# Which chunks of the down projections are done by seven products, and when h is read back

## The chip, the cores and the metric

The kernel runs on one core of a Trainium2 chip. The metric is the device time of one launch in microseconds, the median of several runs. A profile belongs to one execution; its span runs from the first to the last instruction of the core. Engines in the profile are PE (TensorE, matmuls; PEld is its weight load), DVE (VectorE), ACT (ScalarE), POOL (GpSimd) and SP (SyncE, which issues most DMAs).

## The reference

Two layers over x of 256 rows and 1024 columns, all in f32. Each layer is a half-step FFN, a mixer, and a second half-step FFN:

```
def swiglu(h, w_gate, w_up, w_down):
    return (jax.nn.silu(h @ w_gate) * (h @ w_up)) @ w_down

for i in range(DEPTH):                                   # DEPTH = 2, D_MODEL = 1024, D_FF = 2816, SEQ = 256
    h = rmsnorm(x, ffn1_norm[i])
    x = x + 0.5 * swiglu(h, ffn1_w_gate[i], ffn1_w_up[i], ffn1_w_down[i])
    h = rmsnorm(x, mix_norm[i])
    proj = h @ w_in[i]                                   # then self attention (chunked in layer 0,
    ...                                                  # differential in layer 1) and memory attention
    x = x + jnp.concatenate([o_s, o_m], axis=-1) @ w_out[i]
    h = rmsnorm(x, ffn2_norm[i])
    x = x + 0.5 * swiglu(h, ffn2_w_gate[i], ffn2_w_up[i], ffn2_w_down[i])
```

The change is in the FFNs alone. A stage is named (layer, FFN): (0,1), (0,2), (1,1), (1,2).

## The kernel before

**Matmuls in three passes.** Every f32 operand is split into a rounded high part and the rest. `dense` (L503) issues for each product hi·xh (L511), lo·xh (L514, the low part of the weights) and hi·xl (L517), each of 128x512. So each piece of a weight needs a cast on ACT (`hi`, L338, `split_hi`) and a subtraction on VectorE (`lo`, L356, `split_lo`) before TensorE can use it.

**Weights.** `loader` issues the weight DMAs on SP (L294), in the order of use, into three raw buffers. A raw buffer is free again when `split_lo` has read its last piece. The split pieces go to four hi/lo slots, which are free when the last product on them is issued. Items are numbered: in stage (0,2), before and after alike, `lo79` to `lo89` are the eleven chunks 0 to 10 of the down weights, and `lo90` begins the next stage. raw and hi/lo numbers of one chunk differ (raw82 feeds chunk 9, `lo88`).

**The FFN.** Eleven blocks of 256 hidden columns are made first (gate and up, tiles `gu`). `evac` turns each into h: silu on ACT (L633), the product on VectorE (L636), a transpose (L644) into `hb`; then h is written to DRAM (L650, `hd`) and read back in another layout (L656, `hr`), both on SP. A plain chunk splits `hr` into `ht` by a cast (L665) and a subtraction (L667).

**The down stage** has NG = 11 chunks of 256 rows of w_down. Chunks 0 to 7 are taken one by one into four accumulators (`acc00` to `acc11`: two row blocks by two column halves). Chunks 8, 9 and 10 are then taken quarter by quarter: all of acc00 first, so that `finish` (L606) can add it to x while the next quarter runs. In a quarter, TensorE takes two pieces of each chunk, for the first quarter the first and the third.

**Seven products.** A plain chunk is 8 products, 24 matmuls. A chunk listed in `SEVEN` for its stage (L377) is done by a Strassen-like scheme of seven products, 21 matmuls. That needs
- on the weights (`seven_item`, L389): four differences `wsum` on VectorE (L350), seven hi casts and seven lo subtractions in place of four of each. The first seven chunk of a stage uses two hi/lo slots. The later ones are "guests", which put three of their pieces into `gxh`/`gxl`, tiles that belong to the activations elsewhere; one guest at a time;
- on h (`seven_forms`, L672): four small sums `sf` (L681), three casts (L690) and three subtractions (L694). From the third seven of a stage on, they wait in the plan until TensorE has come to the second one;
- after the last seven chunk (`seven_sums`, L710): four of the products have gone into PSUM banks `m1`, `m5`, `m6`, `m7` over all seven chunks of the stage. One copy on ACT (L725, `msum<-m1`), then four additions to x (L714) and four sums (L719) on VectorE bring them into x.

**Who sets the order.** A planner (class Flow) runs when the kernel is built. Threads (`evac`, `split_hi`, `split_lo`, `seven_sums`, ...) yield planned times or conditions, and the instruction that comes due first by its costs is written next. The schedule is manual: each engine runs its instructions in just this order, and waits only for what they need. So a change of the table reorders every engine's queue after it.

Of the kernel before, what the change touches and what calls it, by code (L numbers as in the profile page):

```python
# [26 lines left out]
NG = FF // 256  # L27
# [115 lines left out]
def kernel(  # L143
# [13 lines left out]
    flow = Flow()  # L157
# [125 lines left out]
    def add_chunk(parts, uses=8, w=1):  # L283
        return Item([add_raw(parts)], uses, w)
# [89 lines left out]
    def rows2(w, r):  # L374
        return [(lambda raw: k2(raw), w[r * 256:(r + 1) * 256, :].rearrange("(k p) n -> p k n", p=P))]

    SEVEN = {(0, 1): (), (0, 2): (1, 4, 7), (1, 1): (1, 4, 7), (1, 2): (1, 4, 7)}  # L377
    PAIR = {(0, 1): 4, (0, 2): 3, (1, 1): 3, (1, 2): 3}

    def turned2(w, r):  # L380
        src = w[r * 256:(r + 1) * 256, :].rearrange("(k b i) n -> b i k n", k=2, b=4)
        return [((lambda raw, b=b: k2(raw)[b::4]), src[b]) for b in range(4)]
# [6 lines left out]
    def seven_item(it, guest):  # L389

        r = [it.own(q) for q in range(4)]
        t = lambda j: lambda: it.t[j]
        it.n, it.uses, it.takes, it.gives, it.guest = 1 if guest else 2, 7, 4, 4, guest
        it.sums = [(r[1], r[0]), (r[3], t(0)), (r[3], r[1]), (r[2], t(1))]
        it.units = [(r[0], 0, 1, None), (r[2], 1, 1, None), (r[3], 2, 1, None)] + [(t(j), 3 + j, 1, j) for j in range(4)]
# [46 lines left out]
    def plan_ffn(l, nm, wg, wu, wd):  # L442
# [34 lines left out]
        for c in range(NG):  # L477
            dn.append(add_chunk(turned2(wd[l], c)))
            if c in SEVEN[l, nm]:
                seven_item(dn[-1], c != SEVEN[l, nm][0])  # L480
            elif c >= NG - 3:
# [136 lines left out]
    def ffn(l, nm, xt, gc_next):  # L618
        hts = [None] * NG
        htt = [None] * NG  # L620
        sv = SEVEN[l, nm]
        prog = [-1]

        def evac(g, ps, end, gives=None):


            hb = None
            for tb in range(2):
                yield lambda: end[tb] is not None and xt.rt[tb] is not None
                yield end[tb]  # L630
                yield g2.has(3)
                sil = g2.take([P, 256], F32, "sil")
                nc.scalar.activation(sil, ps[tb][:, 0:256], AF.Silu, scale=xt.r[tb])  # L633
                yield flow.act(256)
                h = g2.take([P, 256], F32, "h")
                nc.vector.scalar_tensor_tensor(out=h, in0=ps[tb][:, 256:512], scalar=xt.r[tb], in1=sil,  # L636
                                               op0=ALU.mult, op1=ALU.mult)
                t = flow.dve(256, 0.06)
                g2.give()
                (gives or (banks, banks))[tb].give()  # L640
                if hb is None:
                    hb = g2.take([P, 4, 2, 2, 32], F32, "hb")
                yield t
                nc.vector.transpose(out=hb[:, :, tb].rearrange("p b f j -> p f b j"),  # L644
                                    in_=h.rearrange("p (f b i) -> p f b i", f=2, b=4))
                t = flow.dve(256, 0.05)
                g2.give()
            yield t
            hd = dram.tile([4, 32, 4, P], F32, tag="hd", name="hd")
            nc.sync.dma_start(out=hd.rearrange("a i b x -> (a i) (b x)"), in_=hb.rearrange("p b t f j -> p (b t f j)"))  # L650
            yield flow.now + 3.0
            g2.give()
            yield flow.now + 2.0
            yield g2.has()
            hr = g2.take([P, 4, P], F32, "hr")
            nc.sync.dma_start(out=hr, in_=hd.rearrange("a i b x -> (i b) a x"))  # L656
            yield flow.now + 6.5
            src = hr.rearrange("p a (c j) -> p c a j", c=4)
            if g in sv:
                yield from seven_forms(g, src)  # L660
                return
            yield g4.has()
            ht = g4.take([P, 2, 4, P], F32R, "ht")
            hi, lo = (ht[:, i].rearrange("p c (a j) -> p c a j", a=4) for i in range(2))
            nc.scalar.copy(out=hi, in_=src)  # L665
            yield flow.act(512)
            nc.vector.tensor_sub(lo, src, hi.bitcast(F32))  # L667
            t = flow.dve(512)
            g2.give()
            hts[g], htt[g] = ht, t  # L670

        def seven_forms(g, src):  # L672


            yield lambda: g4.left >= 2 and g2.left >= 4 and (sv.index(g) < 2 or prog[0] >= sv[1])
            ht = [g4.take([P, 8, P], F32R, "h7") for _ in range(2)]
            sf = g2.take([P, 4, P], F32, "sf")
            s1, s2, s3, s4 = (sf[:, j].rearrange("p (a j) -> p a j", a=4) for j in range(4))
            for op, o, x, y in ((nc.vector.tensor_add, s1, src[:, 2], src[:, 3]), (nc.vector.tensor_sub, s2, s1, src[:, 0]),
                                (nc.vector.tensor_sub, s3, src[:, 0], src[:, 2]), (nc.vector.tensor_sub, s4, src[:, 1], s2)):  # L680
                op(o, x, y)  # L681
                t = flow.dve(P, 0.06)
            yield t
            view = lambda x: x.rearrange("p c (a j) -> p c a j", a=4)
            parts = ((slice(0, 2), src[:, 0:2], view(ht[0][:, 0:2]), view(ht[1][:, 0:2])),
                     (slice(2, 3), src[:, 3:4], view(ht[0][:, 2:3]), view(ht[1][:, 2:3])),
                     (slice(3, 7), sf, ht[0][:, 3:7], ht[1][:, 3:7]))
            ts = []
            for js, x, hi, lo in parts:
                nc.scalar.copy(out=hi, in_=x)  # L690
                ts.append(flow.act(P * (js.stop - js.start)))
            for (js, x, hi, lo), t in zip(parts, ts):
                yield t
                nc.vector.tensor_sub(lo, x, hi.bitcast(F32))  # L694
                t = flow.dve(P * (js.stop - js.start))
            g2.give(2)
            hts[g], htt[g] = ht, t
# [52 lines left out]
        def plain_chunk(g, c, tbs, ks=range(4)):  # L750
            if g not in open_:
                flow.until(banks.has(2))
                open_[g] = [bank(f"gu{tb}", (P, 512)) for tb in range(2)], [None, None]
                flow.spawn(evac(g, *open_[g]))
            ps, end = open_[g]
            for tb in tbs:
                for k in ks:
                    kk = 4 * c + k
                    t = dense(ps[tb], xt.h[tb][:, kk, :], xt.l[tb][:, kk, :], lambda: xt.t[tb][kk],
                              plan[l, nm, "gu"][g, c], k, kk == 0, kk == KT - 1)  # L760
                if c == 1 and 3 in ks:
                    end[tb] = t
# [60 lines left out]
        def product(m):  # L823

            name, left = {"m1": ("b11", (0, 0)), "m5": ("t1", 0), "m7": ("t3", 2), "m6": ("t2", 1), "m3": ("b22", 3),
                          "m2": ("b21", (0, 1)), "m4": ("t4", (1, 1))}[m]
            flow.until(banks.has())
            pb[m] = bank("pair_" + m, (P, 512))
            if m == "m1":
                flow.spawn(pair_sums())  # L830
                for e in range(2):
                    flow.spawn(evac(pair + e, pps[e], pend[e], (g2, g2)))
            for k in range(4):
                if isinstance(left, int):
                    flow.until(lambda: xt.ft[left] is not None)
                    f = xt.fm[left]
                    fh, fl, ready = f[:, 0, k, :], f[:, 1, k, :], lambda: xt.ft[left]
                else:
                    tb, kk = left[0], 4 * left[1] + k
                    fh, fl, ready = xt.h[tb][:, kk, :], xt.l[tb][:, kk, :], lambda: xt.t[tb][kk]  # L840
                t = dense(pb[m], fh, fl, ready, pit[name], k, k == 0, k == 3)
            mt[m] = t
            if m == "m3":
                g4.give(4)
# [874 lines left out]
```

## Time and profile before

| | |
|---|---|
| median of 3 runs | 955.35 us (955.19 to 955.69) |
| profiled execution | 955.69 us, of which the span is 953.9 us |
| mean granted TensorE clock | 1.000 |
| down stage (0,2) begins | 432.70 us after the span's start |
| down stage (1,1) begins | 609.4 us |
| down stage (1,2) begins | 892.3 us |
| SP waiting for VectorE to free a raw buffer | 417.5 us, 110 times |

Times inside the span are counted from its first instruction. A row of the timeline has the start in us, the duration of one instruction or of a run of xN alike instructions, the engine, the line, the operation, out<-in by the program's names, and in brackets the idle time before it with what ended it. VectorE and TensorE start an instruction before the one ahead of it has ended, so a rate is read from start to start, not from a duration.

### The profile page before, as it was taken

The numbers are of one execution on the slowest core, as the hardware profiler recorded it, in microseconds if no ns is written. First come the engines' busy times: TensorE is split into PE (matmuls) and PEld (weight loads), VectorE is DVE, ScalarE is ACT, GpSimd is POOL, SyncE is SP. The second block draws the span as 40 slices with busy tenths as digits, with TensorE's granted clock in tenths as the row PEclk, the third lists the DMA queues.
The fourth block names the chain that finished last, engine by engine and source line by source line (L and its number), as shares of the span: only waits on it lengthen the run. The fifth ranks groups of instructions, "written<-read, shape, count | busy, mean of one in ns | idle before, by whom it ended". The sixth has DMA issues, their size and how long they took to land.

```text
span 953.9 us, 13334 instructions
## 1 busy us (share of the span) xinstructions
PE 945.6 (99%) x4475; PEld 774.1 (81%) x4475; DVE 820.0 (86%) x1483; ACT 587.0 (62%) x1121; POOL 109.1 (11%) x160
## 2 busy tenths in 40 slices
PE   9999999999999999999999999999999999999998
PEld 7888888887777888888888888888787778888886
DVE  7898978888777899979889899796999888999884
ACT  6556566677676746647546656564676865665650
POOL 1000057621210100000000000000434200000000
PEclk9999999999999999999999999999999999999999
DMA  8987799486525387887746679775641367588751
GB/s 265 289 263 236 224 354 296 158 276 210 177 90 177 97 266 225 262 287 219 245 146 219 208 226 288 247 253 166 196 158 57 121 214 228 183 275 276 239 197 45
DMA packets 169887, 204.04 MB, mean 214 GB/s; under 512 B 10137, under 2 KB 145114, under 8 KB 169818
## 3 DMA queue, kind: packets, MB, share of 16 engines
q1 hardware_dynamic: 169498, 202.78, 66.0%
q8 instruction: 35, 0.57, 0.3%
q10 hardware_dynamic: 320, 0.40, 0.1%
q14 instruction: 34, 0.28, 0.1%
HBM read 188.99 MB, written 14.16 MB: 213 GB/s over the span
## 4 chain that ended last, share of the span: by engine, by line
PE 90%; DVE 6%; DMA 2%; ACT 1%; issue 1%; SPq 0%; ACTq 0%; DVEq 0%
PE gu L517 13%; PE gu L514 13%; PE gu L511 13%; PE acc L511 9%; PE acc L517 9%; PE acc L514 9%; PE pair_m L511 3%; PE pair_m L514 3%; PE pair_m L517 3%; PE pj L517 2%; PE pj L511 2%; PE pj L514 2%; DVE lo L356 2%; PE S L1360 1%; DMA x<-in_x_dram 1%; PE AV L1441 1%
## 5 line engine op out<-in xcount | busy, mean ns | idle before, releaser
L338 ACT CAST hi<-raw 128x512 fp32r<-128x512 f32 (+1 forms) x467 | 336.3, 770 | 172.6 <-DMA raw<-in_ffn_w_up_dram 45.6
L356 DVE TENSOR_TENSOR lo<-raw,hi 128x512 fp32r<-128x512 f32 (+1 forms) x467 | 391.9, 875 | 35.5 <-ACT hi L338 35.4
L514 PE MATMUL gu<-lo,xh 128*128 128x512 f32 x576 | 224.7, 390 | 0.5 <-DVE lo L356 0.5
L517 PE MATMUL gu<-hi,xl 128*128 128x512 f32 x576 | 224.5, 390 | 0.4 <-DVE xl L562 0.4
L511 PE MATMUL gu<-hi,xh 128*128 128x512 f32 x576 | 224.4, 390 | 0.0
L517 PEld LDWEIGHTS gu<-hi,xl 128*128 128x128 f32 x576 | 108.1, 188 | 23.9 <-DVE xl L562 1.7
L514 PEld LDWEIGHTS gu<-lo,xh 128*128 128x128 f32 x576 | 108.1, 188 | 23.5 <-DVE lo L356 1.4
L511 PEld LDWEIGHTS gu<-hi,xh 128*128 128x128 f32 x576 | 108.2, 188 | 22.3
L517 PE MATMUL acc<-hi,ht 128*128 128x512 f32 x280 | 109.5, 391 | 0.0
L511 PE MATMUL acc<-hi,ht 128*128 128x512 f32 x280 | 109.2, 390 | 0.0
L514 PE MATMUL acc<-lo,ht 128*128 128x512 f32 x280 | 109.1, 390 | 0.0
L338 ACT CAST hi<-wsum 128x512 fp32r<-128x512 f32 x82 | 47.7, 619 | 26.5 <-DVE wsum L350 26.5
L514 PE MATMUL pj<-lo,xh 128*128 128x512 f32 x160 | 64.0, 400 | 0.0
L517 PE MATMUL pj<-hi,xl 128*128 128x512 f32 x160 | 63.8, 399 | 0.0
L511 PE MATMUL pj<-hi,xh 128*128 128x512 f32 x160 | 63.8, 399 | 0.0
L514 PEld LDWEIGHTS acc<-lo,ht 128*128 128x128 f32 x280 | 52.6, 188 | 10.9
L517 PEld LDWEIGHTS acc<-hi,ht 128*128 128x128 f32 x280 | 52.6, 188 | 10.8
L511 PEld LDWEIGHTS acc<-hi,ht 128*128 128x128 f32 x280 | 52.6, 188 | 10.7
L532 POOL TENSOR_TENSOR xr<-v,nhalf 128x1 f32<-128x1 f32 x12 | 10.3, 861 | 435.1 <-DVE v L530 435.1
L356 DVE TENSOR_TENSOR lo<-wsum,hi 128x512 fp32r<-128x512 f32 x82 | 52.8, 680 | 0.0
L633 ACT ACTIVATE sil<-gu,xr 128x256 f32<-128x256 f32 x72 | 33.7, 468 | 29.8 <-PE gu L517 29.7
L532 POOL TENSOR_TENSOR hf<-v,nhalf 128x8 f32<-128x8 f32 (+1 forms) x20 | 31.4, 1570 | 87.3 <-DVE v L530 78.9
(232 smaller groups left out, 1429.5 us busy)
## 6 DMA issues: line engine op xcount, KB each, us to landing
raw<-in_ffn_w_down_dram SPq DMA_DIRECT2D x176, 256.0 KB, 4.5
raw<-in_ffn_w_gate_dram SPq DMA_DIRECT2D x82, 512.0 KB, 4.0
raw<-in_ffn_w_up_dram SPq DMA_DIRECT2D x82, 512.0 KB, 5.4
raw<-in_w_in_dram SPq DMA_DIRECT2D x32, 512.0 KB, 4.4
hd<-hb SPq DMA_DIRECT2D x44, 256.0 KB, 4.6
hr<-hd SPq DMA_DIRECT2D x44, 256.0 KB, 4.6
raw<-in_w_out_dram SPq DMA_DIRECT2D x8, 1024.0 KB, 5.1
raw<-in_w_mem_kv_dram SPq DMA_DIRECT2D x4, 1024.0 KB, 5.3
```

Of the source, the lines that this page charges most:

```text
L338: nc.scalar.copy(out=it.part(0, q, w), in_=src())
L356: nc.vector.tensor_sub(it.part(1, q, w), src(), it.part(0, q, w).bitcast(F32))
L511: nc.tensor.matmul(out=ps, lhsT=xh, rhs=wh, start=start, stop=False)
L514: nc.tensor.matmul(out=ps, lhsT=xh, rhs=wl, start=False, stop=False)
L517: nc.tensor.matmul(out=ps, lhsT=xl, rhs=wh, start=False, stop=stop)
L532: nc.gpsimd.tensor_tensor(out=dst, in0=v[:, :n], in1=nhalf[:, :n], op=ALU.pow)
L633: nc.scalar.activation(sil, ps[tb][:, 0:256], AF.Silu, scale=xt.r[tb])
L1360: nc.tensor.matmul(out=ss[e][:, pr, :nk], lhsT=q[rows, pr, :], rhs=k[rows, pr, :], start=i == 0, stop=i == len(passes) - 1)
L1441: nc.tensor.matmul(out=av[64 * e:64 * e + 64, pr, :], lhsT=vsrc(kb, pr, e), rhs=pts[e][:, pr, kb, :], start=(kb == 0), stop=(kb == nb - 1))
```

## The change

The table of seven chunks gets one more chunk in each of the three stages that have any, at other places, and `evac` lets the read of h be planned 8 instead of 2 planner-microseconds after the write's buffer is released, for blocks 0 to 7.

```
-    SEVEN = {(0, 1): (), (0, 2): (1, 4, 7), (1, 1): (1, 4, 7), (1, 2): (1, 4, 7)}
+    SEVEN = {(0, 1): (), (0, 2): (1, 2, 4, 6), (1, 1): (1, 2, 4, 6), (1, 2): (1, 3, 5, 7)}
...
             nc.sync.dma_start(out=hd.rearrange("a i b x -> (a i) (b x)"), in_=hb.rearrange("p b t f j -> p (b t f j)"))
             yield flow.now + 3.0
             g2.give()
-            yield flow.now + 2.0
+            yield flow.now + (8.0 if g < NG - 3 else 2.0)
             yield g2.has()
             hr = g2.take([P, 4, P], F32, "hr")
             nc.sync.dma_start(out=hr, in_=hd.rearrange("a i b x -> (i b) a x"))
```

TensorE has 3987 instructions in place of 3996 in the program. How the rows move is seen best at three places.

VectorE at the end of down stage (0,2), before. lo87, lo88 and lo89 are the weights of chunks 8, 9 and 10; x0 and x1 are the two row blocks of x:

```order
L356 TENSOR_TENSOR lo87_0_4776<-raw81_4666,hi87_0_4775 128x512 x4
L356 TENSOR_TENSOR lo88_0_4800<-raw82_4693,hi88_0_4799 128x512 x4
L356 TENSOR_TENSOR lo89_0_4842<-raw83_4786,hi89_0_4841 128x512 x4
L356 TENSOR_TENSOR lo90_0_4884<-raw84_4812,hi90_0_4883 128x1024
L714 SCALAR_TENSOR_TENSOR x0_85<-msum_4888,x0_85 128x512
L719 TENSOR_TENSOR msum_4888<-msum_4888,m6_4548 128x512
```

The same place after:

```order
L356 TENSOR_TENSOR lo87_0_4812<-raw81_4748,hi87_0_4811 128x512 x3
L714 SCALAR_TENSOR_TENSOR x0_85<-msum_4849,x0_85 128x512
L719 TENSOR_TENSOR msum_4849<-msum_4849,m6_4548 128x512
L356 TENSOR_TENSOR lo87_0_4812<-raw81_4748,hi87_0_4811 128x512
L719 TENSOR_TENSOR msum_4850<-msum_4849,m5_4547 128x512
L714 SCALAR_TENSOR_TENSOR x0_85<-msum_4850,x0_85 128x512
L719 TENSOR_TENSOR msum_4849<-msum_4849,m7_4549 128x512
L356 TENSOR_TENSOR lo88_0_4845<-raw82_4801,hi88_0_4844 128x512
L714 SCALAR_TENSOR_TENSOR x1_86<-msum_4849,x1_86 128x512
L719 TENSOR_TENSOR msum_4849<-msum_4849,m5_4547 128x512
L356 TENSOR_TENSOR lo88_0_4845<-raw82_4801,hi88_0_4844 128x512 x3
L714 SCALAR_TENSOR_TENSOR x1_86<-msum_4849,x1_86 128x512
L356 TENSOR_TENSOR lo89_0_4884<-raw83_4837,hi89_0_4883 128x512 x4
```

The eight sums of the seven products stood behind all pieces of the stage's weights; now they stand between the pieces of chunks 8, 9 and 10.

ACT at the same place, before (hi are the casts of the same weights):

```order
L338 CAST hi88_0_4799<-raw82_4693 128x512 x4
L338 CAST hi89_0_4841<-raw83_4786 128x512 x4
L338 CAST hi90_0_4883<-raw84_4812 128x1024
L725 COPY msum_4888<-m1_4546 128x512
```

And after:

```order
L338 CAST hi87_0_4811<-raw81_4748 128x512 x4
L338 CAST hi88_0_4844<-raw82_4801 128x512
L725 COPY msum_4849<-m1_4546 128x512
L338 CAST hi88_0_4844<-raw82_4801 128x512 x3
L338 CAST hi89_0_4883<-raw83_4837 128x512 x4
```

The copy that begins the sums has moved ahead of most of chunk 9's casts, but stands behind the first of them, which needs raw82.

SP in the gate and up part of stage (0,1), as an example of the second edit, before:

```order
L656 DMA hr_620<-hd_562 128x4x128
L294 DMA raw13_647<-in_ffn1_w_gate_dram 128x4x256
L294 DMA raw13_647<-in_ffn1_w_up_dram 128x4x256
L310 DMA grow_146<-in_a_q_norm_dram 1x64
L650 DMA hd_673<-hb_602 128x512
```

And after:

```order
L294 DMA raw13_644<-in_ffn1_w_gate_dram 128x4x256
L294 DMA raw13_644<-in_ffn1_w_up_dram 128x4x256
L310 DMA grow_146<-in_a_q_norm_dram 1x64
L650 DMA hd_670<-hb_611 128x512
L656 DMA hr_678<-hd_559 128x4x128
```

The read of one block of h has moved behind the next weight loads and the next block's write.

More of the change, by code (lines that the diff above doesn't have):

```diff
@@ L375, in rows2 @@
         return [(lambda raw: k2(raw), w[r * 256:(r + 1) * 256, :].rearrange("(k p) n -> p k n", p=P))]
-    SEVEN = {(0, 1): (), (0, 2): (1, 4, 7), (1, 1): (1, 4, 7), (1, 2): (1, 4, 7)}
+    SEVEN = {(0, 1): (), (0, 2): (1, 2, 4, 6), (1, 1): (1, 2, 4, 6), (1, 2): (1, 3, 5, 7)}
     PAIR = {(0, 1): 4, (0, 2): 3, (1, 1): 3, (1, 2): 3}
@@ L652, in evac @@
             g2.give()
-            yield flow.now + 2.0
+            yield flow.now + (8.0 if g < NG - 3 else 2.0)
             yield g2.has()
```

## The prediction

> **What bounds the kernel now.** I read the page first (share of each engine, granted clock, the chain), then the three stages that the change touches as time windows, then the waits, then the timelines of those stages.
>
> ```profile
> span 953.9 us, 13334 instructions
> PE 945.6 (99%) x4475; PEld 774.1 (81%) x4475; DVE 820.0 (86%) x1483; ACT 587.0 (62%) x1121; POOL 109.1 (11%) x160
> PE 90%; DVE 6%; DMA 2%; ACT 1%; issue 1%; SPq 0%; ACTq 0%; DVEq 0%
> ```
>
> TensorE is busy 99% of the span, and the chain that ended last is 90% TensorE. So each matmul taken away is worth its pitch, as long as nothing makes TensorE wait. VectorE, at 86%, is the next to fill up.
>
> The windows of the three changed down stages ((0,2), (1,1), (1,2); the columns are busy time and count of PE, PEld, DVE, ACT, POOL, then clock, DMA share, GB/s):
>
> ```profile
> 432.70:489.60 56.90, 56.90 (x258) 47.17 (x257) 48.20 (x84) 30.84 (x58) 0.33 (x1) 1.00 0.67 212
> 609.40:666.30 56.90, 56.90 (x259) 47.14 (x257) 48.83 (x85) 32.62 (x63) 0.00 (x0) 1.00 0.66 210
> 892.30:950.30 58.00, 57.92 (x256) 47.65 (x254) 43.63 (x77) 25.91 (x50) 0.00 (x0) 1.00 0.46 150
> ```
>
> TensorE never stops in them, at a granted clock of 1.00, and VectorE already has 48 of 57 us busy in the first two. There is no TensorE wait to win, only matmuls; and VectorE has about 8 us of room, which is what the change spends.
>
> **What a chunk costs TensorE.** First matmul of chunk 0 of stage (0,2), and the next chunk's first:
>
> ```profile
> 432.70 0.39 PE L511 MATMUL acc<-hi,ht 128*128 128x512 f32 x1
> ...
> 438.14 0.39 PE L511 MATMUL m<-hi,h 128*128 128x512 f32 x1
> ```
>
> 24 matmuls in 438.14 − 432.70 = 5.44 us, 0.2267 us each (the 0.39 us overlap). A seven chunk has 21: 4.76 us, 0.68 less. The change makes one more seven chunk in each of three stages: 9 matmuls, −2.04 us. This is the whole gain on offer.
>
> **What a seven chunk costs VectorE.** One, with its forms, in the same stage of before:
>
> ```profile
> 453.62 0.28 DVE L681 TENSOR_TENSOR sf<-hr 128x128 f32<-128x128 f32 x1
> ...
> 454.55 0.68 DVE L350 TENSOR_TENSOR wsum<-raw 128x512 f32<-128x512 f32 x1
> 455.27 0.69 DVE L350 TENSOR_TENSOR wsum<-raw,wsum 128x512 f32<-128x512 f32 x1
> 455.88 0.62 DVE L694 TENSOR_TENSOR h<-hr,h 128x256 fp32r<-128x256 f32 x2
> ...
> 458.22 1.89 DVE L356 TENSOR_TENSOR lo<-raw,hi 128x512 fp32r<-128x512 f32 x3
> 460.03 0.69 DVE L356 TENSOR_TENSOR lo<-wsum,hi 128x512 fp32r<-128x512 f32 x1
> 460.63 1.89 DVE L356 TENSOR_TENSOR gxl<-wsum,gxh 128x512 fp32r<-128x512 f32 x3
> 462.44 3.73 DVE L356 TENSOR_TENSOR lo<-raw,hi 128x512 fp32r<-128x512 f32 x6
> ```
>
> Starts back to back are 0.60 us apart for a 128x512 operation (458.22 to 460.03 holds three; 0.603 over longer runs), although one takes 0.68; a difference that reads the one just before it starts 0.72 after it (454.55 to 455.27). The four sf take 0.93, the pair of narrow L694 0.54. So a seven chunk takes 462.44 − 453.62 = 8.82 us of VectorE, a plain one 4 × 0.603 (lo) + 0.60 (L667) = 3.0: 5.8 us more VectorE to save 0.68 us of TensorE.
>
> The Trainium skill, "VectorE: DVE Perf Modes", section "The DRAIN you can't avoid", says that the next operation does not start until the pipe of the one before has emptied. The trace does not show that here: the next starts 0.08 us before the end of the one before. By the rule, at least 0.685 an operation, the saturated stretch below would be 5.5 us longer in each of two stages.
>
> **Where VectorE stands at the end of stage (0,2)** (T = 432.70), before: chunk 10's lo pieces, then TensorE's first use of one of them, and the sums after the sevens:
>
> ```profile
> 470.32 2.50 DVE L356 TENSOR_TENSOR lo<-raw,hi 128x512 fp32r<-128x512 f32 x4 [2.94 <-ACT hi L338]
> ...
> 477.13 0.39 PE L514 MATMUL acc<-lo,ht 128*128 128x512 f32 x1
> ...
> 473.29 0.58 ACT L725 COPY msum<-m 128x512 f32<-128x512 f32 x1
> ...
> 474.57 0.68 DVE L714 SCALAR_TENSOR_TENSOR x<-msum,x 128x512 f32<-128x512 f32 x1
> ```
>
> All lo pieces are done at 472.8, 4.3 us before chunk 10's first L514 (477.13 = T+44.43); the eight sums (L714, L719) come behind them. In the changed order the last seven chunk is 6 instead of 7, so the sums become due one chunk earlier and stand between the pieces of chunks 8, 9 and 10. They are 8 × 0.603 = 4.8 us in front of lo89, more than the whole lead, and with the fourth seven's 5.8 us ahead of them too.
>
> **The tally of VectorE, after, (0,2).** TensorE wants chunk 9's first two lo at T+42.4 and 43.07, chunk 10's at 43.75 and 44.43 (before's uses less the 0.68 of one more seven). VectorE's queue becomes solid when it has the last gate/up product of the stage:
>
> ```profile
> 433.99 0.46 ACT L633 ACTIVATE sil<-gu,xr 128x256 f32<-128x256 f32 x1
> ...
> 435.22 0.48 DVE L636 SCALAR_TENSOR_TENSOR h<-gu,xr,sil 128x256 f32<-128x256 f32 x1
> 435.62 0.68 DVE L356 TENSOR_TENSOR lo<-raw,hi 128x512 fp32r<-128x512 f32 x1
> 436.22 0.44 DVE L644 STREAM_TRANSPOSE hb<-h 128x256 f32<-128x256 f32 x1
> 436.58 0.65 DVE L356 TENSOR_TENSOR lo<-raw,hi 128x512 fp32r<-128x512 f32 x1
> ```
>
> L636 takes 0.40 and L644 0.36 of the queue. The silu started at T+1.29 because ACT was at casts; without that it ends about T+0.7. I take VectorE's start as T+1.25, an estimate between T+0.7 and the T+2.5 of this row's L636. From there to lo87's third piece the new order has 52 operations of 128x512 (12 wsum, 36 lo and gxl, 2 L667, 2 wide L694): 31.4 us, plus L636 0.40, L644 0.36, two sf sets 1.86, two narrow L694 pairs 1.08, three dependent waits of 0.12: 1.25 + 35.4 = T+36.7. Until there every chunk's pieces come over 1 us ahead of TensorE.
>
> The next operation is L714, which needs ACT's L725, and in ACT's new queue the first cast of hi88 stands ahead of L725. That cast needs raw82, the raw buffer freed by lo85's last raw piece, the 41st wide operation: T+30.0. How long a freed buffer takes to come back as a cast, in before (release, load, cast):
>
> ```profile
> 439.04 2.50 DVE L356 TENSOR_TENSOR lo<-raw,hi 128x512 fp32r<-128x512 f32 x4 [1.21 <-ACT hi L338]
> ...
> 441.56 2.53 SPq L294 DMA_DIRECT2D raw<-in_ffn_w_down_dram  x4
> ...
> 448.78 0.63 ACT L338 CAST hi<-raw 128x512 fp32r<-128x512 f32 x1 [1.89 <-DMA raw<-in_ffn_w_down_dram]
> ```
>
> 448.78 − 441.54 = 7.25 us. So hi88 starts at T+37.25, L725 ends about T+38.4 (cast and copy at 0.52 to 0.58 each), and VectorE has idled 1.8 us. From T+38.5 on, by the new order: lo88's first piece is done at 42.9, its third (the second that TensorE takes) at 45.3, lo89's first at 47.1, its third at 48.3. TensorE then waits 0.5, 1.75, 1.1 and 0.5 us: **S = 48.3 − 44.43 = 3.85 us**. If the reload is early enough to hide, 1.8 less: S ≈ 2.1. If VectorE is 2 us ahead of my count as well, 0; with its start at T+2.5, 5.
>
> Stage (1,1) has the same order: the same S. In (1,2), sevens 1, 3, 5, 7, only the first two sums precede chunk 10's first lo: 60 wide operations, it is done at T+42.2 against 43.75; its third piece, with 64, is done at 44.7 against 44.43. I count 0 (between 0 and 0.5, since before's VectorE idles in that place) and keep the gain of 0.68.
>
> **The distance of the read of h.**
>
> ```profile
> SPq L294 <- DVE lo L356: 417.5, 110, 21.9
> SPq L656 <- DMA hd<-hb: 50.1, 22, 4.7
> ```
>
> (Queue, awaited, us in all, times, longest.) The read waited on its write 22 times, 50.1 us of SP's queue, with weight loads behind it. But SP's weight loads wait far longer for VectorE's release of a buffer (417.5 us), and TensorE waits for neither, so I count 0 for the gain. What it costs: each L665 and L667 pair comes about one gate/up chunk later, and one more L667 lies in the down stage (in the 52). Were weight loads really freed by it, each of the reload times above could shrink by the wait of up to 4.7 us; that is the no-idle case (S ≈ 2.1). Were h late for TensorE, chunk 0 would show it: at most 1 or 2 us a stage, taken at 0 because two further chunks' h stand between.
>
> The other stages:
>
> ```profile
> 680.00:785.00 105.00, 102.67 (x574) 81.44 (x573) 94.00 (x197) 73.03 (x192) 30.71 (x26) 1.00 0.44 142
> ```
>
> The layer-1 mixer is the one place where TensorE idles (2.3 us of 105). The new plan reorders its instructions without adding any: ±1 us, taken as 0.
>
> **Sum.** −2.04 + 2 × 3.85 = +5.7. The profiled execution of before took 955.69 (span 953.9, 1.8 around it), 0.34 above the median; on the median, 955.35 + 5.66 = **961.0 us**, with the ends of S at 0 and 5. About 0.2% (1.9 us) is what a measurement of this kernel can tell from no change.
>
> **Rivals.**
> - *All hidden* (S = 0): VectorE starts its solid stretch earlier or its reload is faster, and the 9 matmuls come out whole: 955.35 − 2.04 = 953.3, faster. For it: VectorE idles in the old stage (2.94 us ahead of chunk 10's lo). Against: the sums alone use up the 4.3 us lead. It decides where VectorE is 4 us ahead of my count. 0.11.
> - *Small stall*: the reload hides and VectorE is 0.6 us ahead: S ≈ 1.5, 955.35 − 2.04 + 3.0 = 956.3, no difference that can be told. 0.25.
> - *The forecast*, S of 2.1 to 5: 957.5 to 963.3, at 961.0. 0.51.
> - *More*: waits spread to chunks 3 to 7, since the third and fourth seven hold a wsum and two form slots, or the mixer's new order loses: 964 to 967. 0.10.
> - *The clock drops* in the hold. In before the granted clock is 1.00 even in the window with 2.3 us of idling, and my waits come in pieces of up to 1.75 us. One slow stretch of 3.4 us, at half speed, would add 1.7 in each of two stages: 964.3. 0.02. The Trainium skill, "TensorE: Matmul & The Clock Gate", Part 1, puts the switch to half rate at an idle window of about 3.4 us; no row of before shows one.
> - *Each VectorE operation waits for the pipe to empty*: 5.5 more in S twice, 972; the pitch of 0.60 speaks against it. 0.01.
>
> **Chances and range.** Faster by over 0.2%: nearly the whole of the first rival, 0.10. Within: its rest and the small stall, with the lower edge of the forecast, 0.28. Slower: 0.62. From 953.2 to 963.8 leaves out the last three cases and a little of the first; the forecast's own range is 957.5 to 963.3.
>
> **What would show it.** In the changed profile: 9 matmuls fewer at 0.2267; TensorE L514 acc waiting on VectorE's lo near 475 to 479 and again some 182 us later, in three or four pieces and about 3.9 us a stage; L714 on VectorE idling for ACT's L725 about 1.8 us, with hi88 waiting on the load of w_down just ahead of it; the last stage without a wait; SP's wait on hd nearly gone, without effect. The forecast is wrong if VectorE comes to lo87 before T+35, or if raw82's cast starts before T+35.5; then the sums are done in time.

## The result, and the profile after

The changed kernel takes 967.48 us in the median (966.61 to 968.30), against 955.35 before. The ratio of the runs, which is not quite that of the medians, is 1.0121, interval 1.0110 to 1.0133. The profiled execution took 967.58 us. The page of after, its span, busy shares and chain:

```profile
span 965.4 us, 13340 instructions
PE 948.4 (98%) x4466; PEld 772.8 (80%) x4466; DVE 835.7 (87%) x1522; ACT 595.5 (62%) x1136; POOL 110.6 (11%) x160
PE 51%; DVE 25%; DMA 14%; ACT 5%; issue 3%; SPq 2%; DVEq 0%; ACTq 0%
```

The 9 matmuls are gone (4475 to 4466), but the chain is no longer one wall of TensorE: a quarter of it is VectorE. The windows of the three changed stages, each from its first matmul to the first of what follows (columns as before):

```profile
433.90:499.10 65.20, 61.67 (x266) 49.23 (x265) 58.51 (x103) 38.56 (x72) 0.55 (x1) 0.97 0.59 190
616.50:680.30 63.80, 61.11 (x266) 49.26 (x265) 57.99 (x106) 39.06 (x76) 0.55 (x1) 0.97 0.60 194
902.90:961.70 58.80, 57.81 (x253) 46.92 (x251) 50.21 (x91) 30.00 (x58) 0.00 (x0) 1.00 0.44 144
```

In the first two, TensorE stands for 3.5 and 2.7 us by this count, and the granted clock is 0.97 instead of 1.00. All runs, by stage: the table has the time from a stage's first matmul to the next stage's first, read from the timelines of TensorE (us), and the ratio of the runs to before; e10 stands further down.

| kernel | (0,2) | (1,1) | (1,2) | mixer 1 | ratio (interval) |
|---|---|---|---|---|---|
| before | 59.3 | 59.3 | 58.0 | 105.5 | 1 |
| after | 65.2 | 63.8 | 58.8 | 104.9 | 1.0121 (1.0110 to 1.0133) |
| e1 table only | 66.4 | 63.7 | 57.3 | 104.9 | 1.0113 (1.0098 to 1.0129) |
| e2 read only | 59.3 | 59.3 | 58.0 | 105.8 | 1.0008 (0.9998 to 1.0018) |
| e3 after, sums late | 61.7 | 64.4 | 57.3 | 104.6 | 1.0069 (1.0056 to 1.0083) |
| e4 table only, sums late | 65.0 | 69.6 | 57.3 | 104.4 | 1.0128 (1.0113 to 1.0142) |
| e5 (1,4,6) twice | 59.3 | 59.3 | 58.0 | 104.9 | 0.9997 (0.9986 to 1.0008) |
| e6 (1,3,5,7) | 58.6 | 58.6 | 57.3 | 106.7 | 0.9992 (0.9983 to 1.0001) |
| e7 (1,2,4,7) | 60.4 | 61.0 | 62.5 | 108.6 | 1.0126 (1.0109 to 1.0143) |
| e8 after, h split later | 61.1 | 61.0 | 59.2 | 104.9 | 1.0044 (1.0030 to 1.0057) |
| e9 e8 with sums late | 59.6 | 59.9 | 57.3 | 106.0 | 1.0029 (1.0016 to 1.0043) |
| e11 (1,3,5,7), (1,4,6), (1,3,5,7) | 58.6 | 59.3 | 57.3 | 104.9 | 0.9988 (0.9980 to 0.9997) |
| e12 (1,3,5,7), (1,4,7), (1,3,5,7) | 58.6 | 59.3 | 57.3 | 104.9 | 0.9986 (0.9977 to 0.9995) |

After is 5.9, 4.5 and 0.8 us longer in the three stages, 0.7 shorter in the mixer, 0.4 shorter in the gate and up part of (1,2), and 1.2 longer ahead of (0,2), where TensorE waited 1.3 us for x and 0.8 for a gate load in that execution (0.3 and 0 in before). The end of stage (0,2) on TensorE, after (in brackets the wait, with what ended it):

```profile
477.39 0.39 PE L511 MATMUL acc<-hi,ht 128*128 128x512 f32 x1
478.19 0.50 PE L514 MATMUL acc<-lo,ht 128*128 128x512 f32 x1 [0.41 <-DVE lo L356]
...
480.11 0.50 PE L514 MATMUL acc<-lo,ht 128*128 128x512 f32 x1 [0.95 <-DVE lo L356]
...
482.52 0.64 PE L514 MATMUL acc<-lo,ht 128*128 128x512 f32 x1 [1.45 <-DVE lo L356]
482.96 0.63 PE L517 MATMUL acc<-hi,ht 128*128 128x512 f32 x1
483.38 0.63 PE L511 MATMUL acc<-hi,ht 128*128 128x512 f32 x1
```

Three waits, for chunk 9's two lo pieces and chunk 10's first. From start to start they cost 0.57, 1.12 and 1.62 us over the usual pitch: 3.3 in all. Then matmuls start 0.427 us apart instead of 0.227, eight of them. The windows of the hold and of what follows, in (0,2), (1,1) and (1,2):

```profile
477.40:482.50 5.10, 2.31 (x8) 0.97 (x6) 5.07 (x10) 3.28 (x6) 0.00 (x0) 1.00 0.63 198
482.50:486.00 3.50, 3.48 (x9) 2.70 (x10) 3.50 (x6) 0.89 (x1) 0.00 (x0) 0.53 0.94 297
658.80:663.90 5.10, 2.41 (x9) 1.02 (x8) 5.07 (x10) 4.59 (x9) 0.00 (x0) 0.97 0.58 187
663.90:667.30 3.40, 3.40 (x9) 2.68 (x10) 3.21 (x6) 0.60 (x2) 0.00 (x0) 0.54 1.00 310
946.00:949.50 3.50, 2.54 (x11) 1.50 (x10) 3.46 (x7) 0.13 (x1) 0.00 (x0) 1.00 0.00 0
```

While TensorE stands, VectorE is busy 5.07 of 5.10 us: it is the engine that is late, not a transfer. Behind the two longer holds the granted clock is 0.53 and 0.54 for about 3.4 us, some 1.7 us each. Behind the short one of the last stage nothing follows. Two more holds of 0.5 us lie in the middle of (0,2), at chunks 3 and 4. VectorE at the stage's start and at its sums, after, with one row of ACT:

```profile
433.57 0.62 ACT L665 CAST ht<-hr 128x512 fp32r<-128x512 f32 x1 [4.26 <-DMA hr<-hd]
...
434.23 0.69 DVE L667 TENSOR_TENSOR ht<-hr,ht 128x512 fp32r<-128x512 f32 x1 [2.45 <-ACT ht L665]
...
437.36 0.48 DVE L636 SCALAR_TENSOR_TENSOR h<-gu,xr,sil 128x256 f32<-128x256 f32 x1
...
473.52 0.69 DVE L714 SCALAR_TENSOR_TENSOR x<-msum,x 128x512 f32<-128x512 f32 x1 [0.87 <-ACT msum L725]
...
477.45 0.68 DVE L356 TENSOR_TENSOR lo<-raw,hi 128x512 fp32r<-128x512 f32 x1
...
479.37 1.89 DVE L356 TENSOR_TENSOR lo<-raw,hi 128x512 fp32r<-128x512 f32 x3
...
481.78 3.62 DVE L356 TENSOR_TENSOR lo<-raw,hi 128x512 fp32r<-128x512 f32 x5
```

The L667 is that of chunk 8's h. TensorE wants it 41 us into the stage, but it stands early in VectorE's queue, and its h is still in flight: VectorE idles 2.45 us. ACT stands 4.26 us at the cast of the same h (L665), with the last block's silus behind it. So the last L636 comes at T+3.5 (T = 433.9 here). In (1,1), where a like wait of 2.54 us ends 0.8 us ahead of the stage's first matmul, it comes at T+2.3.

Each of TensorE's three waits ends 0.74 us after the start of the lo row that it needs: 477.45 and the first of 479.37's three for chunk 9, the first of 481.78's five for chunk 10.

### The profile page after: what moved, and what is told of

The parts are those of the page before. It is cut to its first block, busy times and chain, and to the rows that moved or that the text cites. A ratio compares the mean times of both kernels' runs of the same rounds, so it can differ in the third digit from the quotient of the medians.

```text
span 965.4 us, 13340 instructions
## 1 busy us (share of the span) xinstructions
PE 948.4 (98%) x4466; PEld 772.8 (80%) x4466; DVE 835.7 (87%) x1522; ACT 595.5 (62%) x1136; POOL 110.6 (11%) x160
## 3 DMA queue, kind: packets, MB, share of 16 engines
q1 hardware_dynamic: 169498, 202.78, 65.2%
## 4 chain that ended last, share of the span: by engine, by line
PE 51%; DVE 25%; DMA 14%; ACT 5%; issue 3%; SPq 2%; DVEq 0%; ACTq 0%
DVE lo L356 11%; PE gu L514 7%; PE gu L517 7%; PE gu L511 7%; DMA raw<-in_ffn_w_up_dram 7%; DMA raw<-in_ffn_w_down_dram 4%; DVE wsum L350 4%; PE acc L514 3%; PE acc L517 3%; PE acc L511 3%; ACT hi L338 3%; PE pj L517 3%; PE pj L514 3%; PE pj L511 3%; SPq L294 2%
## 5 line engine op out<-in xcount | busy, mean ns | idle before, releaser
L514 PE MATMUL acc<-lo,ht 128*128 128x512 f32 x256 | 102.3, 399 | 6.8 <-DVE lo L356 6.8
L517 PE MATMUL acc<-hi,ht 128*128 128x512 f32 x256 | 101.2, 395 | 0.0
L511 PE MATMUL acc<-hi,ht 128*128 128x512 f32 x256 | 101.2, 395 | 0.0
L338 ACT CAST hi<-wsum 128x512 fp32r<-128x512 f32 x85 | 50.6, 621 | 56.7 <-DVE wsum L350 52.0
L514 PEld LDWEIGHTS acc<-lo,ht 128*128 128x128 f32 x256 | 48.8, 191 | 20.5 <-DVE lo L356 10.7
L511 PEld LDWEIGHTS acc<-hi,ht 128*128 128x128 f32 x256 | 48.8, 191 | 10.3
L517 PEld LDWEIGHTS acc<-hi,ht 128*128 128x128 f32 x256 | 48.8, 191 | 9.8
```

What stands on the lines that cost most here:

```text
L338: nc.scalar.copy(out=it.part(0, q, w), in_=src())
L511: nc.tensor.matmul(out=ps, lhsT=xh, rhs=wh, start=start, stop=False)
L514: nc.tensor.matmul(out=ps, lhsT=xh, rhs=wl, start=False, stop=False)
L517: nc.tensor.matmul(out=ps, lhsT=xl, rhs=wh, start=False, stop=stop)
```

## The experiments

**e1 and e2: each edit alone.**

```
e1   SEVEN as changed;   yield flow.now + 2.0
e2   SEVEN as before;    yield flow.now + (8.0 if g < NG - 3 else 2.0)
```

> The table of seven chunks as changed, the read of h at its old distance. Theory 'late read': in the changed kernel VectorE idles 2.45 us (stage (0,2)), 2.54 (1,1) and 3.53 (1,2) on an L667 whose hr came late; these put its queue 2.5 to 3.5 us behind. With the old distance that idling goes, the holds at the end of the first two stages shrink from 3.4 to about 0.5 to 1 us, the granted clock stays at 1.00, the hold of 1.4 us in the last stage and the two of 0.6 us in the middle of (0,2) go: about 955 to 956.5 us. Theory 'sums and the fourth seven alone' (the reading does nothing): the same holds, the same clock, 966 to 968.

Measured 966.75 us: the table alone loses as much as the whole change. But in the profiled execution the clock stays at 1.00, and the holds are distributed in another way: 3.7 us in the middle of (0,2), 1.8 in (1,1), and 2.74 at the end of each. The last L636 comes at T+7.9 in (0,2) and T+5.4 in (1,1). The L667 that VectorE waits for is there with the old distance too:

```profile
433.31 0.69 DVE L667 TENSOR_TENSOR ht<-hr,ht 128x512 fp32r<-128x512 f32 x1 [2.84 <-ACT ht L665]
```

So the distance of the read does not make that wait; "late read" as I had put it fell, and so did "the same holds".

> The old table of seven chunks, the read of h at its new distance. Both theories: VectorE idles at the start of the stages if the read comes late, but with three sevens it has 4 us and more of lead at the end of each stage, so TensorE does not see it: 955.4 within 1 us. If the read alone costs TensorE time somewhere (an L667 needed by chunk 0 to 2), 957 and more.

Measured 957.15 against 956.09, no difference that can be told; every down stage as before. VectorE idles 3.0 to 3.8 us at an L667 ahead of each of the three stages, and TensorE does not see it.

**e3 and e4: the sums behind chunk 10's pieces**, with the change whole and with the table alone.

```
             yield t
+            yield lambda: None not in dn[NG - 1].lot[:4]
             yield g2.has(2)
             u, w = (g2.take([P, 512], F32, "msum") for _ in range(2))
```

> The changed kernel whole, but the copy L725 and the eight sums L714 and L719 are planned only when all lo pieces of chunk 10 are. Theory 'sums': the end holds (3.4 us in each of two stages, 1.4 in the last) and the slow clock behind them (1.9 and 1.75) go; left are the two holds of 0.6 in the middle of (0,2), which come from the late start: about 955.5 to 957. Theory 'late read': the eight sums are 4.8 us of the queue and lo89 comes 4.8 us earlier, against 3.4 needed: also without end holds. The two do not differ here; what is tested is that the holds and the clock hang together. Should the clock stay low without the holds, it has another cause.

> The new table, the old distance of the read, and the sums after chunk 10's pieces. If both theories hold, no hold is left in the down stages and the 9 matmuls come out whole: 955.35 - 2.04 = 953.3, within 0.7. If the fourth seven's VectorE work itself (5.8 us a stage) holds TensorE in mid-stage, 954 to 956.

e3: 963.47; e4: 968.50. No lo is late at the end of e3's stages, but the time comes back one step later. The longest wait of e3, in (1,1), the next stage's transpose for x:

```profile
662.50 0.95 PE L525 MATMUL xtp<-ident,x 128*128 128x128 f32 x4 [3.74 <-DVE x L714]
```

Behind it the clock falls as in after. The work that stood ahead of lo now stands ahead of x. In (1,1) moving the sums only moves the wait; in (0,2) one wait of 2.16 us is left at the end, the clock holds, and the stage is 3.5 us shorter than after. In e4, with the mid-stage holds of e1 besides, it is worse. There the clock falls in (1,1) behind a single wait of 2.54 us:

```profile
670.99 0.66 PE L525 MATMUL xtp<-ident,x 128*128 128x128 f32 x4 [2.54 <-DVE x L714]
...
672.95 0.63 PE L511 MATMUL acc<-hi,ht 128*128 128x512 f32 x1
673.38 0.63 PE L514 MATMUL acc<-lo,ht 128*128 128x512 f32 x1
```

Seven matmuls start 0.427 us apart there. My expectation of 955.5 to 957 and of 953.3 missed this.

**e5, e6, e7: which sevens.** Before, with only the table changed:

```
e5   (0, 2): (1, 4, 6),     (1, 1): (1, 4, 6),     (1, 2): (1, 4, 7)
e6   (0, 2): (1, 3, 5, 7),  (1, 1): (1, 3, 5, 7),  (1, 2): (1, 3, 5, 7)
e7   (0, 2): (1, 2, 4, 7),  (1, 1): (1, 2, 4, 7),  (1, 2): (1, 2, 4, 7)
```

> Before with chunks 1, 4 and 6 in stages (0,2) and (1,1): three sevens as before (no fewer matmul), but the last one a chunk earlier, so that the sums stand between the pieces of chunks 9 and 10. Theory 'place of the sums': they alone bring most of the end holds, 2 to 3.4 us in each of two stages: 959 to 964. Theory 'VectorE's sum of work': without the fourth seven's 5.8 us VectorE has room for the sums in that place: holds under 0.7 us, 955.5 to 957.

> Before with chunks 1, 3, 5 and 7 in all three stages (old distance of the read): four sevens spread out, the last at 7. Theory 'VectorE's sum of work': the fourth seven fills VectorE wherever it stands; as the sums come at chunk 10's pieces, holds of 1 to 3 us in (0,2) and (1,1), 955 to 958. Theory 'places': with the sums behind chunk 9 and no two sevens side by side TensorE is not held: 953.3 (all 9 matmuls won).

> Before with chunks 1, 2, 4 and 7 in all three stages: the side-by-side sevens of the change with the last at 7. If the early pair (1, 2) is what puts VectorE behind in mid-stage: the mid-stage holds of the table alone (4.0 us in (0,2), 1.8 in (1,1)) come, and as VectorE has chunks 5 and 6 to recover, no end holds of over 1 us: 957 to 960. If only the early sums matter: 953.5 to 954.5.

e5: 955.70, no hold in (0,2) and (1,1): with three sevens, sums between the pieces of chunks 9 and 10 cost nothing. (Its profiled execution was 2.5 us over the median, with a longer wait in stage (0,1).) e6: 955.76, and all three down stages 0.7 us shorter without one wait: a fourth seven is not too much for VectorE when the sevens are spread. But the 2.0 us do not arrive; the layer-1 mixer is 1.2 longer. A wait there that came to 0.7 us in before (two times) comes to 1.9 in e6's waits (engine, line, awaited, us, times, longest):

```profile
PE qktp L525 <- DVE m L1266: 1.9, 2, 1.4
```

e7: 968.65, 12.9 us slower than e6, with the same number of sevens and the same last one. Its waits:

```profile
PE m L514 <- DVE lo L356: 4.5, 4, 1.4
PE S L1360 <- ACT PT L1374: 1.6, 1, 1.6
PE acc L514 <- DVE lo L356: 1.6, 3, 1.1
```

The holds lie at chunks 1 to 4, 1.6 us in (0,2), 2.0 in (1,1), 4.2 in (1,2), as in e1; at the end of the stages there are none. So they come with the early sevens 1, 2 and 4, and not with the early sums. What e6 and e7 do not separate is the order from VectorE's start: the L667 idles 2.04 and 2.08 us just ahead of (0,2) and (1,1) in e7 and not in e6, and the last L636 comes at T+5.2 to T+8.5 against T+2.1 to T+2.6. Over all traces with sevens at 1 and 2, the mid-stage holds grow with that time: none up to T+2.3, 1.05 us at T+3.5 (after), 1.56 at T+5.2 (e7), 3.7 at T+7.9 (e1). e7 is also 3.0 us longer than before in the mixer and 1.4 in the gate and up part of (1,2), which I had not expected. That e7 is as slow as after is a coincidence of different holds.

**e8: VectorE not kept waiting for h.**

```
-            yield flow.now + 6.5
+            yield flow.now + (14.0 if sv and g in (3, 8, 9, 10) else 6.5)
```

> The changed kernel, with the cast and the subtraction of h of blocks 3, 8, 9 and 10 (L665, L667) planned 7.5 planner-us later, the read itself where it was. VectorE then no longer stands 2.45 to 3.5 us at an L667 whose h is still in flight at the start of each stage. Theory 'late h': its queue is 2.5 us ahead, the mid-stage holds of 1.2 us go, the end holds of 3.4 shrink to under 1.5, the clock stays at 1.00: 955.5 to 959. Theory 'sum of work and the reload' (the tally on record, which had VectorE start without that idling): end holds of 2 to 3.9 remain: 960 to 966.

Measured 960.41: 7 us of the 12 are gone. The last L636 of the stage, now (T = 433.0):

```profile
434.80 0.48 DVE L636 SCALAR_TENSOR_TENSOR h<-gu,xr,sil 128x256 f32<-128x256 f32 x1 [0.47 <-ACT sil L633]
```

T+1.8 instead of T+3.5. The mid-stage holds are gone, those at the end are 0.66 + 0.41 + 1.01 = 2.1 us in (0,2) and the same in (1,1), 1.65 in (1,2), and the clock is 1.00 throughout. VectorE comes to L714 at T+35.9 without idling. The size is that of the tally's case "no idle", S = 2.1, in both stages, but the case is not quite that one: the edit also moved the first of the sums two lo pieces forward. So even without the L667's wait, the four sevens at 1, 2, 4, 6 with the sums in between hold TensorE.

**e9: e8 with e3's edit.** In this kernel one of the eight sums of (1,1) is added to x0 after that part of x has been taken to the mixer; the instructions are all there. The transpose for x in (1,1) therefore waits for less than it should.

> The changed kernel with both: h of blocks 3, 8, 9, 10 split later, and the sums planned behind chunk 10's pieces. Theory 'two causes, one queue' (the idling on L667 and the pair 1, 2 hold TensorE in mid-stage; the sums ahead of chunks 9 and 10 hold it at the end): no hold in the middle and none on lo; what is left of the 2.1 us at the end comes as one wait of the next stage's transpose for x, under 1.5 us a stage: 953.5 to 956.5, clock 1.00. Theory 'VectorE's sum of work is too much in any order': the end hold of 2.1 comes back whole, at the transpose: 958 to 961.

Measured 958.76. No lo is late; the transposes for x wait 0.96 and 1.10 us over their pitch. In the down stages it is as "two causes, one queue" has it, at most one wait of under 1.5 us a stage (59.6, 59.9, 57.3), with the reserve just made for (1,1). But the mixer and the gate and up part of (1,1) are 1.2 and 0.8 us longer than in e8, and the whole lands in the other theory's range, 958 to 961, by losses which neither theory has.

**e10: the clock.** e1 with one lo subtraction of chunk 10 repeated, once in (0,2) and twice in (1,1):

```
-                nc.vector.tensor_sub(it.part(1, q, w), src(), it.part(0, q, w).bitcast(F32))
+                again = 0 if q else 1 if it is plan[0, 2, "dn"][NG - 1] else 2 if it is plan[1, 1, "dn"][NG - 1] else 0
+                for _ in range(1 + again):
+                    nc.vector.tensor_sub(it.part(1, q, w), src(), it.part(0, q, w).bitcast(F32))
```

> The new table alone (old distance of the read), where chunk 10's first lo subtraction is done twice in stage (0,2) and three times in (1,1); the same values are written again, TensorE's work is the same. Its end holds were 1.13 + 1.61 = 2.74 us in 3.5 us with the granted clock at 1.00 behind them. One more subtraction makes them 3.35 in (0,2), two 3.95 in (1,1). Theory 'the clock drops when TensorE stands over about 3 us in a stretch of 5': both stages run 8 or 9 matmuls at 0.427 us behind the hold, 1.75 to 1.9 us each; in all 966.75 + 0.6 + 1.2 + 3.6 = about 972. Theory 'the drop in the changed kernel had another cause': 968.5, clock 1.00.

Measured 971.51 (ratio 1.0159, 1.0143 to 1.0175), 4.8 us over e1, of which 1.8 are the subtractions. The windows of e1's holds and of what follows:

```profile
480.20:484.40 4.20, 1.80 (x7) 0.84 (x6) 4.17 (x8) 2.72 (x6) 0.00 (x0) 1.00 0.47 159
484.40:488.00 3.60, 3.60 (x16) 2.98 (x17) 3.60 (x6) 0.88 (x1) 0.00 (x0) 1.00 1.01 331
661.40:665.60 4.20, 1.79 (x7) 0.84 (x6) 4.17 (x8) 3.85 (x8) 0.00 (x0) 1.00 0.54 176
665.60:669.00 3.40, 3.40 (x18) 2.75 (x18) 3.40 (x7) 1.56 (x3) 0.00 (x0) 1.00 0.96 303
```

And of e10's:

```profile
478.80:483.90 5.10, 1.97 (x7) 1.01 (x7) 5.03 (x9) 3.61 (x6) 0.00 (x0) 0.87 0.53 172
483.90:489.20 5.30, 5.30 (x13) 4.14 (x14) 4.37 (x6) 0.00 (x0) 0.00 (x0) 0.50 0.93 311
664.60:670.10 5.50, 1.71 (x6) 0.73 (x5) 5.40 (x10) 5.19 (x10) 0.00 (x0) 1.00 0.62 198
670.10:674.00 3.90, 3.85 (x10) 3.05 (x11) 3.83 (x7) 0.15 (x1) 0.00 (x0) 0.56 0.69 215
```

The holds are 3.95 us in (0,2) and 4.2 in (1,1), more than the 3.35 and 3.95 expected. The same kernel, with one or two VectorE operations more: the clock falls to half where it had stayed, and its mean is 0.995 to 0.996 in all four executions, against 1.000, 0.998, 0.998 and 1.000 in e1's. So longer holds bring the fall. Where it begins, e1 does not show: 0.998 is also the mean in the traces of e3 and e4, which have one slow stretch each, so in two of e1's executions it probably fell once, with the same order of instructions. (The mean alone is no proof: one of 22 executions of before has 0.997.)

**e11 and e12: the best of the stages put together**, before with

```
e11  (0, 2): (1, 3, 5, 7),  (1, 1): (1, 4, 6),  (1, 2): (1, 3, 5, 7)
e12  (0, 2): (1, 3, 5, 7),  (1, 1): (1, 4, 7),  (1, 2): (1, 3, 5, 7)
```

> Spread sevens: (1, 3, 5, 7) in (0,2) and (1,2), (1, 4, 6) in (1,1), old distance of the read. By the stages measured apart: 0.68 each won in (0,2) and (1,2), no hold in (1,1), and the layer-1 mixer with the order that comes of (1, 4, 6), 104.9 us against 105.5: 955.35 - 1.36 - 0.6 = 953.4. If the mixer's 104.9 does not come back, 954.0.

> As the last, with (1, 4, 7) in (1,1) as before. The down stages 58.6, 59.3 and 57.3; the layer-1 mixer as in before, 105.5: 955.35 - 1.36 = 954.0. With (1, 3, 5, 7) in (1,1) too, all three stages were 0.7 shorter but the mixer 1.3 longer; if that came from (0,2) and not from (1,1), it comes here as well: 955.3.

Measured 954.48 and 955.04, against 955.94 for before in the same runs: 0.12% (0.03 to 0.20) and 0.14% (0.05 to 0.23) faster. TensorE of e11 in its three down stages:

```profile
433.40:492.00 58.60, 58.60 (x265) 48.51 (x264) 54.53 (x96) 34.62 (x65) 0.00 (x0) 1.00 0.61 200
609.40:668.70 59.30, 59.30 (x269) 49.06 (x268) 51.06 (x91) 34.68 (x67) 0.55 (x1) 1.00 0.64 208
891.30:948.60 57.30, 57.28 (x253) 47.13 (x251) 48.09 (x87) 28.11 (x55) 0.00 (x0) 1.00 0.43 142
```

No stop in any of them. VectorE at 54.5 of 58.6 us shows how little is left. In e12 the mixer does not lose what it lost in e6, so that loss came of (1, 3, 5, 7) in (1,1), the stage just ahead of it. (By the medians e11 is the faster of the two, by the ratios e12.) These two are the versions that beat both kernels, by little.

## Why the prediction was wrong

The direction and the place were right: 1.2% slower, with TensorE waiting for VectorE's lo at chunks 9 and 10, in three pieces, in both stages. The size was not: +5.66 forecast, +12.1 measured, above the range.

- **The 9 matmuls, −2.04: right.** Stage (1,2) of e1 and e3, and all three of e6, are 0.7 shorter.
- **The end holds, S = 3.85 in each of two stages: mechanism right, one term mis-sized.** 3.3 and 3.2 measured. The tally took the second piece that TensorE wants of chunks 9 and 10 as the third of its chunk in VectorE's queue; it is the second, as the wait that ends behind 479.37 shows. With one operation of 0.60 us less ahead of it, the tally's own times give 0.5 + 1.1 + 1.7 and no fourth wait: 3.35 us. In (1,1) VectorE came to L714 at T+38.4, against T+38.5 forecast. In (0,2) it came at T+39.6, after idling 0.87 us for L725 instead of 1.8, and TensorE was itself 1.3 us later by its mid-stage holds. That the two delays cancel there is luck.
- **VectorE's start, T+1.25 with ends at T+0.7 and T+2.5: failed in (0,2).** It was T+3.5 there and T+2.3 in (1,1). I counted what VectorE does after the last L636 and not what it waits for before it. Such a wait stood in the trace of before, 3 us ahead of the stage:

```profile
429.68 0.69 DVE L667 TENSOR_TENSOR ht<-hr,ht 128x512 fp32r<-128x512 f32 x1 [1.75 <-ACT ht L665]
```

  In the new order it moved behind the stage's start. Hence the holds in mid-stage (1.05 us in (0,2)) that I had excluded with "over 1 us ahead". e8 takes the wait away and finds these holds gone and S at 2.1.
- **The clock: the step that failed with most weight, a term left out of the sum.** I priced it right (1.7 a stage) and gave it 0.02, since no single wait of mine was over 1.75 us. It came in both stages, 3.4 us in all, more than half of what the forecast missed. The longest wait does not decide it: it was 1.43 us in (1,1) of after, with the fall, and 1.44 in (0,2) of e1, without. A forecast of 3.85 us of standing within 6 us made it likely; it belonged to the forecast's own sum, not beside it as a rival. The Trainium skill, "TensorE: Matmul & The Clock Gate", Part 1, has the clock fall after an idle window of about 3.4 us. The traces here differ: in after, waits of 0.4 to 1.5 us with three matmuls between them were enough, and in e4 one of 2.54 us.
- **(1,2), counted 0 to 0.5: 1.5.** Here two sums stand ahead of chunk 10's first lo and two more ahead of its second, as I had read, but VectorE had the first done at about T+43.8 instead of T+42.2. The L667 that idles 3.53 us ahead of this stage does not explain it alone: e8 has the same order of sums, no such idling, and a hold of 1.65. In e1, with the old distance of the read, both pieces stand ahead of all the sums, and the stage has no hold. So the distance did cost 1.5 us in this stage, by the order that the planner made of it, and only together with the new table. What made VectorE late in that order, no run takes apart.
- **The distance of the read: right as to 0** by itself (e2).
- **The mixer, 0 ± 1: −0.7**, inside. The +1.2 us ahead of (0,2) are in loads; that the change has no part in them is not shown, but (0,2) begins anywhere from 432.7 to 435.8 us in the other traces.

Sum: −2.04 + 3.3 + 3.2 (end holds) + 1.05 (mid (0,2)) + 0.7 (the matmul behind a wait, which starts 0.34 instead of 0.23 us after it, six times) + 1.5 (end (1,2)) + 3.4 (clock) − 0.7 (mixer) − 0.4 (gate and up of (1,2)) = +10.0; with the 1.2 of the start 11.2, of the 11.5 by which the span grew.

The rivals: "small stall" and "all hidden" are out. "More" (964 to 967) was nearest in time and named a spread to chunks 3 to 7, but that spread is the smaller part of what came. "The clock drops" had the mechanism of the larger part, at the lowest chance but one. That each VectorE operation waits for the pipe to empty is out: the three lo from 479.37 to the next start at 481.18 are 0.60 us apart.

What stays open besides: why the sevens 1, 2, 4, 7 also lengthen the mixer in e7, and why (1, 3, 5, 7) in (1,1) does so by 1.2 us. The planner's order there changes with the table; no run took it apart.

## What to carry to other kernels

Where one engine is the bound and another is 86% busy, the second engine's queue must be followed from before the stage begins, waits included: an operation that nobody needs yet, standing early in an in-order queue with its data in flight, costs as much as the work, once that queue has no room left (e2 has such waits too, with three sevens, and loses nothing). Read the order inside a merged row before counting on it. Count the whole standing of TensorE in a stretch, not the longest wait: the holds of some 3.2 us here brought the clock down and so cost half as much again. Work traded from the bound engine to a nearly full one was won here only when it was spread (1, 3, 5, 7 against 1, 2, 4, 7: the same products, 12.9 us apart, 9.5 of them in the three down stages).

## What the hardware showed that was not expected

The granted clock can fall behind a sum of short waits: in after, 3.3 us of standing in 5.1, in three waits of 0.57, 1.12 and 1.62, was followed by 0.53 for 3.5 us. Holds of 2.74 us in 4.2 were followed by no fall in the trace of e1, twice, nor were those of 2.1 in e8. But no single figure divides the cases: e4 has the fall behind one wait of 2.54 us, with TensorE busy 2.46 of the 5.0 us up to its end, and e1's own mean clock differs from execution to execution. Over which stretch the standing counts, and from when, these runs do not show. The length of the slow stretch varies: 3.4 us in after, 5.3 in e10's (0,2).
